# A feed-forward product by seven half-size block products, with loads and gates moved

## The chip, the cores and the metric

One core of one Trainium2 chip runs the whole kernel as one program. The metric is the device time of one execution in microseconds (us). The engines are TensorE (PE), which multiplies matrices into the PSUM banks; VectorE (DVE); ScalarE (ACT); GpSimd (POOL), which has no access to PSUM; and SyncE (SP), which only starts transfers. Each engine has an instruction queue of its own and goes through it in order; waits between engines are semaphores. PEld is the loading of weights into PE, which overlaps the matmuls.

## The reference

Two transformer-like layers over 1024 tokens of width 1024, in float32. What matters here is the first layer:

```python
    xn = _rmsnorm(h, norm_mix_w[l]);  proj = xn @ w_in[l]
    attn = _windowed_gqa(...)         # 8 heads, a band of +-128 keys
    gdn = _gdn_mixer(...)             # gated delta rule in chunks, forward and backward
    h = h + jnp.concatenate([attn, gdn], axis=-1) @ w_out[l]
    hn = _rmsnorm(h, norm_ffn_w[l])
    h = h + jnp.square(jax.nn.relu(hn @ w_ffn_in[l])) @ w_ffn_out[l]
```

Here w_ffn_in is 1024 x 4096 and w_ffn_out 4096 x 1024. The second layer projects its normed input to three branches (pooling, a short convolution, a stick-breaking attention) and to a gate of 3 x 1024 columns; each branch is multiplied with its weights of 512 x 1024, then with sigmoid(gate); the sum goes through w_out_2, a norm, and is added to the layer's input.

## The kernel before

Every matrix operand is held as two float32r tiles, a rounded part H and a remainder L (`split`, L97: ACT casts, DVE or POOL subtracts). A product of a 128x128 block with a 128x512 tile is three matmuls, H.H, H.L and L.H (`mm3`, L146 to L150). Weights come in 256 KB pieces (`weight`, L103): SP loads `raw` (three buffers), ACT casts it, POOL makes the remainder; the w tiles have eight buffers each. `cols` and `rows` cut the weights of a product, `dense` runs one: 24 matmuls fill a PSUM bank, then an epilogue reads it.

The order within an engine's queue is made at build time by a planner that simulates the queues; the order in the program is its priority. Only in the stick-breaking attention is PE's order written out by hand (`turns`, with other products as `fill` between). Loads go through SP's queue (`dma`), most stores through ACT's (`put`). Both are in order: a load that waits for a buffer holds up those behind it. Tile pools are opened and closed in program order, and a new pool may lie over the memory of closed ones; a tile in it waits for the old tiles under it.

The stages in order of time, as far as the change touches them:

- Chunk loop (150 to 260 us). For each of 8 chunks `chunk_of` loads kT and qT, and `decay` loads e, with a copy one chunk ahead. PE transposes kT (L459) and multiplies kT with kT and with qT; ACT and POOL make the decays in e, which has two buffers; the results go to DRAM (`key_d`, `qry_d`). Other projections fill PE.
- Inversion (260 to 331 us). DVE inverts 32x32 blocks row by row (L510, L511), ACT copies X to Xr (L512), four stores bring it to DRAM (L515). PE runs projections.
- Attention and scan (338 to 560 us). The scan's first steps load X and B (L581), then KQ and kv. The attention loads bias (L716), KR (L720) and, per block, R (L729), from which ACT and POOL make Q (L731, L732); L737 is its first matmul. Both run interleaved.
- Output projection (560 to 676 us), which ends with a loop over 8 token tiles in the order 3, 4, 2, 5, 1, 6, 0, 7. Its results `Hs` stay in SBUF.
- Norm and feed-forward (642 to 1345 us). `to_units` scales a token tile (L181), PE transposes it (L184), ACT and DVE split it (L187, L188). Then eight rounds c: the first product for 512 hidden columns, relu and square on ACT (L866, L867), a split (`hid`), and the second product, added to `Hs` on DVE (L881).
- The second layer. Its gate products for the first two branches are fill in the stick-breaking attention and go through DRAM (`ga_d`); 24 parts of the fill are kept back for its end (SPARE). From 2130 us on the three branches follow: y is loaded (`yr`, two buffers) and split, the last branch's gates are computed (two of eight early, the others inside the loop), products and gates are multiplied.
- The last product and norm (2400 to 2472 us): L1282 squares, `rstd_from` makes the factor (L171 to L173), L1292 scales, L1293 adds the residual.

## Time and profile before

| | us |
|---|---|
| median of 3 runs | 2472.67 (2468.53 to 2473.35) |
| profiled execution | 2473.5 |
| its span, from first to last instruction | 2471.7 |
| PE busy | 2357.5 |
| DVE, ACT, POOL busy | 1220.8, 1140.5, 942.1 |

A group of instructions in a profile is named by line of the kernel, engine, operation, and output<-inputs by the program's tile names. Matmuls overlap, so the duration of one is longer than its share of PE's time. PEclk is the granted clock of TensorE as a part of 2.4 GHz.

### The profile page before, as it was taken

To read this page: it belongs to the slowest core of one execution; us is meant where nothing else is said; L and a number is where in the kernel's file an instruction comes from. 1 tells how busy PE (TensorE), PEld (TensorE's weight loads), DVE (VectorE), ACT (ScalarE), POOL (GpSimd) and SP (SyncE) were. 2 spreads that over 40 slices of the span, in tenths; PEclk is the share of its full clock that TensorE was granted. 3 is DMA by queue.
4 is the path that set the end of the run, shared out by engine and by line. 5 is a ranking of instruction groups with operands and counts; after the bars stand their busy time and mean duration, and the time that the engine had idled before them with its cause. 6 is when DMAs were issued, how large, how long until landed. Compare 5 with 4: busy or idle time off the path is not lost. (4 is left out here: it accounts for less than half of the span.)

```text
span 2471.7 us, 31486 instructions
## 1 busy us (share of the span) xinstructions
PE 2357.5 (95%) x11098; PEld 1955.2 (79%) x11098; DVE 1220.8 (49%) x2221; ACT 1140.5 (46%) x2359; POOL 942.1 (38%) x815
## 2 busy tenths in 40 slices
PE   7988978999999999999999999999999999899998
PEld 5776758898788888888888788777887888787887
DVE  4768846975632211221222601887888776432213
ACT  4646335754642232223224522776666788521331
POOL 3445233434522222222213313465445443326454
PEclk9999978999999999999999999999999999999999
DMA  4657774667121111111112324222212332444123
GB/s 133 184 175 219 212 204 137 188 198 239 58 63 54 41 45 52 51 52 52 48 38 81 118 81 129 63 86 77 77 50 72 99 97 85 145 141 145 56 73 124
DMA packets 301137, 262.17 MB, mean 106 GB/s; under 512 B 44871, under 2 KB 236291, under 8 KB 300979
## 3 DMA queue, kind: packets, MB, share of 16 engines
q1 hardware_dynamic: 258131, 207.12, 28.8%
q10 hardware_dynamic: 42848, 53.05, 6.2%
q8 instruction: 87, 1.43, 0.3%
q14 instruction: 71, 0.58, 0.1%
HBM read 197.63 MB, written 64.57 MB: 106 GB/s over the span
## 5 line engine op out<-in xcount | busy, mean ns | idle before, releaser
L99 POOL TENSOR_TENSOR wl<-raw,wh 128x512 fp32r<-128x512 f32 x260 | 349.2, 1355 | 794.2 <-ACT wh L98 784.8
L148 PE MATMUL mm<-uh,wh 128*128 128x512 f32 x1472 | 577.4, 393 | 5.0 <-ACT mx L157 3.5
L150 PE MATMUL mm<-uh,wl 128*128 128x512 f32 x1472 | 575.8, 391 | 0.0
L149 PE MATMUL mm<-ul,wh 128*128 128x512 f32 x1472 | 575.7, 391 | 0.0
L98 ACT CAST wh<-raw 128x512 fp32r<-128x512 f32 x260 | 160.1, 620 | 437.2 <-PE mm L150 235.1
L148 PEld LDWEIGHTS mm<-uh,wh 128*128 128x128 f32 x1472 | 277.4, 189 | 61.5 <-ACT mx L157 3.9
L150 PEld LDWEIGHTS mm<-uh,wl 128*128 128x128 f32 x1472 | 276.9, 188 | 58.9
L149 PEld LDWEIGHTS mm<-ul,wh 128*128 128x128 f32 x1472 | 277.2, 188 | 55.2
L99 DVE TENSOR_TENSOR hid<-t,hid 128x512 fp32r<-128x512 f32 x64 | 55.3, 866 | 302.8 <-ACT hid L98 302.8
L150 PE MATMUL mm<-wh,hid 128*128 128x512 f32 x512 | 199.0, 389 | 0.0
L149 PE MATMUL mm<-wl,hid 128*128 128x512 f32 x512 | 198.8, 389 | 0.0
L148 PE MATMUL mm<-wh,hid 128*128 128x512 f32 x512 | 198.7, 389 | 0.0
L881 DVE TENSOR_TENSOR h<-h,mm 128x512 f32<-128x512 f32 x128 | 87.8, 687 | 213.1 <-PE mm L150 213.0
L1051 POOL TENSOR_TENSOR ul<-u,uh 128x512 fp32r<-128x512 f32 (+3 forms) x96 | 107.7, 1123 | 158.4 <-ACT uh L1050 147.8
L111 POOL TENSOR_TENSOR wl<-raw,wh 128x512 fp32r<-128x512 f32 x88 | 122.4, 1392 | 117.7 <-DVE wh L110 42.8
L148 PE MATMUL mm<-xnh,wh 128*128 128x512 f32 x352 | 142.2, 404 | 9.7 <-ACT t L310 5.5
L149 PE MATMUL mm<-xnl,wh 128*128 128x512 f32 x352 | 140.6, 400 | 0.0
L150 PE MATMUL mm<-xnh,wl 128*128 128x512 f32 x352 | 140.6, 399 | 0.0
L150 PEld LDWEIGHTS mm<-wh,hid 128*128 128x128 f32 x512 | 96.1, 188 | 19.9
L148 PEld LDWEIGHTS mm<-wh,hid 128*128 128x128 f32 x512 | 96.1, 188 | 19.9
L149 PEld LDWEIGHTS mm<-wl,hid 128*128 128x128 f32 x512 | 96.1, 188 | 19.9
L866 ACT ACTIVATE t<-mm 128x512 f32<-128x512 f32 x64 | 38.1, 597 | 143.3 <-PE mm L150 143.3
(336 smaller groups left out, 4625.4 us busy)
## 6 DMA issues: line engine op xcount, KB each, us to landing
raw<-in_w_in SPq DMA_DIRECT2D x172, 256.0 KB
raw<-in_w_ffn_in SPq DMA_DIRECT2D x64, 256.0 KB
raw<-in_w_ffn_out SPq DMA_DIRECT2D x64, 256.0 KB
raw<-in_w_out SPq DMA_DIRECT2D x32, 256.0 KB
kv<-kv_d SPq DMA_DIRECT2D x16, 512.0 KB
ga_d<-mx ACTq DMA_DIRECT2D x32, 256.0 KB
s<-ga_d SPq DMA_DIRECT2D x32, 256.0 KB
raw<-in_w_branch SPq DMA_DIRECT2D x24, 256.0 KB
```

The lines of the kernel that those rows point to most:

```text
L98: act.copy(H, src)
L99: (eng or dve).tensor_sub(L, src, f32(H))
L111: gp.tensor_sub(L, raw, f32(H))
L148: pe.matmul(ps, A[0][:, asl], B[0][:, bsl], start=first, stop=False)
L149: pe.matmul(ps, A[0][:, asl], B[1][:, bsl], start=False, stop=False)
L150: pe.matmul(ps, A[1][:, asl], B[0][:, bsl], start=False, stop=last)
L866: act.activation(t, ps, AF.Relu)
L881: dve.tensor_add(Hs[order[p], n], Hs[order[p], n], ps)
L1051: gp.tensor_sub(uL[:, cs], u[:, cs], f32(uH[:, cs]))
```

## The change

Feed-forward: the normed input, transposed, is cut in four blocks B00, B10 (first 512 tokens, lower and upper half of the 1024 features), B01, B11 (last 512 tokens); 256 columns of the weights likewise in A00, A01, A10, A11, each 512 x 128. Four block products come from seven multiplications with sums of blocks (T1 to T4 of the input, S1 to S4 of the weights). `half` does the first two, which need only the first 512 tokens, `strassen` the other five. Five groups of 16 have their first two done early, one behind each norm tile from the fourth on (`early`). All hidden tiles go to DRAM (`hid_d`), as does the residual (`h_d`). Then the second product runs on its own in eight rounds and reads them back. PSUM has 6 + 2 banks in place of 4 + 2, raw weight buffers are 4 of double size, block tiles have 14 buffers.

Front loads: `front` loads kT, qT and e together, one chunk ahead. Xr is copied on DVE; its stores, the loads of the scan's first step, and the attention's first loads go through ACT's queue. Gates: SPARE is gone; the last branch's eight gate products stand before the products of the branches (two, three and three), and go through DRAM; `yr` has four buffers. Last norm: the weight is multiplied in before the factor is known.

The diff, cut to its core (in the branch stage, `s` has six buffers):

```diff
-    def decay(c):
...
+    def front(c):
+        kT, qT = chunk_of(gk_d, c, "kT"), chunk_of(gq_d, c, "qT")
         e = up_tile("e", 2)
...
         dma(e, g4.partition_broadcast(P))
...
+        return kT, qT, e
+    ahead = [front(0)]
...
-        kT, qT = chunk_of(gk_d, c, "kT"), chunk_of(gq_d, c, "qT")
+        kT, qT, e = ahead.pop()
+        if c < 7:
+            ahead.append(front(c + 1))
...
-        e = decays.pop(c)
-        if c < 7:
-            decays[c + 1] = decay(c + 1)
...
-        act.copy(Xr, X.rearrange("p j i -> p i j"))
+        dve.tensor_copy(Xr, X.rearrange("p j i -> p i j"))
         for b in range(4):
             r = slice(32 * b, 32 * b + 32)
-            dma(xbq_d[0][d].rearrange("c h i j -> (c h) i j")[:, r, r], Xr[r])
+            put(xbq_d[0][d].rearrange("c h i j -> (c h) i j")[:, r, r], Xr[r])
...
-            dma(by_head(t), xbq_d[n][d][c].rearrange("h i j -> i h j"))
+            (dma if step else put)(by_head(t), xbq_d[n][d][c].rearrange("h i j -> i h j"))
...
-        dma(KQ, xbq_d[2][d][c].rearrange("h i j -> i h j"))
+        first = dma if step else put
+        first(KQ, xbq_d[2][d][c].rearrange("h i j -> i h j"))
         kv = ld.tile([P, 2, 512], F32, name="kv", tag="kv", bufs=KV)
-        dma(kv, kv_d[c].rearrange("n i j -> i n j"))
+        first(kv, kv_d[c].rearrange("n i j -> i n j"))
...
-        dma(bias, bass.AP(w.tensor, w.offset + 127, [[511, P], [P * 512, 4], [1, 384]]))
+        first = dma if kv else put
+        first(bias, bass.AP(w.tensor, w.offset + 127, [[511, P], [P * 512, 4], [1, 384]]))
...
-            dma(KR[64 * s : 64 * s + 64], ka_d[kv * 64 : kv * 64 + 64, :])
+            first(KR[64 * s : 64 * s + 64], ka_d[kv * 64 : kv * 64 + 64, :])
...
-                dma(R[64 * s : 64 * s + 64].rearrange("p (h t) -> p h t", h=4), src)
+                (dma if kv or n > 1 else put)(R[64 * s : 64 * s + 64].rearrange("p (h t) -> p h t", h=4), src)
...
+    rwc.close()
+    rw[:] = pool(rwc, "raw2", 4), 1024
...
-    pm[0] = pool(pf, "pff", 4, space=PSUM)
...
+    pm[0] = pool(pf, "pff", 6, space=PSUM)
...
+    h_d, hid_d = scratch("h_d", [T, 1024]), scratch("hid_d", [4096, T])
...
+    xsp = pool(s5, "xs", 14)
...
+    EARLY = 5
...
+    def spare(name):
+        return hp.tile([P, 512], F32, name=name, tag="h")
...
+    B00f, B10f = xtile("x00", F32), xtile("x10", F32)
...
+    def halved(U, cs, src, eng):
+        act.copy(U[0][:, :, cs], src)
+        eng.tensor_sub(U[1][:, :, cs], src, f32(U[0][:, :, cs]))
+    def operand(src, eng):
+        H, L = (wp.tile([P, 512], F32R, name=f"w{q}", tag=f"w{q}", bufs=8).rearrange("p (k m) -> p k m", k=4) for q in "hl")
+        act.copy(H, src)
+        eng.tensor_sub(L, src, f32(H))
+        return H, L
...
+    def accumulate(ps, A, B, first):
+        for k in range(4):
+            for n, (x, y) in enumerate(((0, 0), (0, 1), (1, 0))):
+                pe.matmul(ps, A[x][:, k], B[y][:, k], start=first and k + n == 0, stop=k == 3 and n == 2,
+                          skip_group_check=not first)
...
+    def sums(A, st):
+        A00, A01, A10, A11 = A
+        S1, S2 = st(), st()
+        dve.tensor_add(S1, A10, A11)
+        dve.tensor_sub(S2, S1, A00)
+        return A, S2, operand(S2, dve), operand(S1, dve)
...
+    def half(c0, A00, A01, mu, ht):
+        pa, pb_ = acc512(), acc512()
+        accumulate(pa, operand(A00, gp), B00, True)
+        m1 = mu("m1")
+        act.copy(m1, pa)
+        accumulate(pb_, operand(A01, gp), B10, True)
+        hidden(pb_, m1, c0, 0, ht)
+        return pa
+    def hidden(ps, other, row, h, ht):
+        t = ht("ht")
+        dve.tensor_add(t, other, ps)
+        dve.scalar_tensor_tensor(t, t, 0.0, t, op0=ALU.max, op1=ALU.mult)
+        put(hid_d[row : row + P, 512 * h : 512 * h + 512], t)
...
+    def early(g):
+        if g == 0:
+            W0[:] = A = blocks_of(F1, 0)
+        else:
+            raw = raw_tile().rearrange("p (k m) -> p k m", k=8)
+            dma(raw, F1[:, 256 * g : 256 * g + P].rearrange("(k p) m -> p k m", p=P))
+            A = raw[:, 0:4], raw[:, 4:8]
+        first.append(half(256 * g, *A[:2], spare, spare))
...
+    for p, i in enumerate(order):
...
+        for j in range(2):
+            put(h_d[i * P : (i + 1) * P, 512 * j : 512 * j + 512], hv[j])
+            xs = tmp()
+            dve.scalar_tensor_tensor(xs, hv[j], rs, wb[:, 512 * j : 512 * j + 512], op0=ALU.mult, op1=ALU.mult)
...
+        if p < 4:
+            if p == 0:
+                B00, B10 = pair("b00"), pair("b10")
+            for U, Uf, src in ((B00, B00f, pq[0]), (B10, B10f, pq[1])):
+                act.copy(Uf[:, :, cs], src)
+                halved(U, cs, src, dve)
+            if p == 3:
+                early(0)
...
+        if p == 4:
+            T1, T2, B11, T3, T4 = (pair(n) for n in ("t1", "t2", "b11", "t3", "t4"))
+        b11, t1, t2, t3, t4 = (tx() for _ in range(5))
+        act.copy(b11, pq[1])
+        dve.tensor_sub(t1, pq[0], B00f[:, :, cs])
+        dve.tensor_sub(t3, b11, pq[0])
+        halved(B11, cs, pq[1], dve)
+        gp.tensor_sub(t2, b11, t1)
+        halved(T2, cs, t2, gp)
+        dve.tensor_sub(t4, B10f[:, :, cs], t2)
+        halved(T1, cs, t1, dve)
+        halved(T3, cs, t3, gp)
+        halved(T4, cs, t4, dve)
+        early(p - 3)
+    sums0 = sums(W0, tx)
+    txc.close()
+    hpc.close()
...
+    def strassen(g):
+        c0 = 256 * g
+        if g == 0:
+            pa, ((A00, A01, A10, A11), _, O2, O1) = first[g], sums0
+            S2 = st()
+            gp.tensor_add(S2, A10, A11)
+            gp.tensor_sub(S2, S2, A00)
+        else:
+            A = blocks_of(F1, c0)
+            pa = first[g] if g < EARLY else half(c0, *A[:2], mu, ht)
+            (A00, A01, A10, A11), S2, O2, O1 = sums(A, st)
+        accumulate(pa, O2, T2, False)
+        u2 = mu("u2")
+        act.copy(u2, pa)
+        pc = acc512()
+        accumulate(pc, O1, T1, True)
+        S3, S4 = st(), st()
+        dve.tensor_sub(S3, A00, A10)
+        accumulate(pa, operand(S3, gp), T3, False)
+        u3 = mu("u3")
+        act.copy(u3, pa)
+        hidden(pc, u3, c0 + P, 1, ht)
+        pd = acc512()
+        accumulate(pd, operand(A11, dve), T4, True)
+        hidden(pd, u3, c0 + P, 0, ht)
+        dve.tensor_sub(S4, A01, S2)
+        accumulate(pc, operand(S4, dve), B11, False)
+        hidden(pc, u2, c0, 1, ht)
+    for g in range(16):
+        strassen(g)
+    f1.close()
+    s5.close()
+    rwc.close()
+    ptc.close()
+    pf.close()
...
+    hid = pool(s5, "hid", 22)
+    wbp = pool(s5, "normw", 1)
...
...
-        to_units(hv, rstd_of(hv), p, wb, HU, [pt.tile([P, 512], F32, name="g", tag="g") for _ in range(2)])
...
+    Hs = {}
+    tiles = [(n, p) for n in range(2) for p in range(8)]
...
-        def f1_epi(m, h, ps):
-            t = tmp()
-            act.activation(t, ps, AF.Relu)
-            act.activation(t, t, AF.Square)
-            D[m, h] = tuple(hid.tile([P, 512], F32R, name="hid", tag="hid") for _ in range(2))
-            split(*D[m, h], t)
-        if c == 0:
-            dense(F1, 0, 1, HN, f1_epi, by_half=True)
-        else:
-            for j in range(2):
-                dense(F1, 512 * c + 256 * j, 2, HN, lambda m, h, ps, j=j: f1_epi(2 * j + m, h, ps))
+        for k in range(4):
+            raw = hid.tile([P, 1024], F32, name="hr", tag="hr", bufs=3)
+            dma(raw, hid_d[(4 * c + k) * P : (4 * c + k + 1) * P, :])
+            for h in range(2):
+                D[k, h] = tuple(hid.tile([P, 512], F32R, name="hid", tag="hid") for _ in range(2))
+                split(*D[k, h], raw[:, 512 * h : 512 * h + 512])
...
-        for n, p in [(n, p) for n in range(2) for p in range(8)] if c < 7 else [(n, p) for p in range(8) for n in range(2)]:
...
-            dve.tensor_add(Hs[order[p], n], Hs[order[p], n], ps)
+            if c == 0:
+                Hs[order[p], n] = hp.tile([P, 512], F32, name="h", tag="h")
+                act.copy(Hs[order[p], n], ps)
+            else:
+                dve.tensor_add(Hs[order[p], n], Hs[order[p], n], ps)
...
+        for n, p in tiles[4 * (c - 2) : 4 * (c - 1)] if 2 <= c < 6 else ():
+            r = tmp()
+            dma(r, h_d[order[p] * P : (order[p] + 1) * P, 512 * n : 512 * n + 512])
+            gp.tensor_add(Hs[order[p], n], Hs[order[p], n], r)
...
-    AHEAD, LEAD, SPARE = 16, 24, 24
...
+    AHEAD, LEAD = 16, 24
...
-            while turn[1] and done < LEAD + (t + 1) / len(turns) * (total - LEAD - SPARE):
+            while turn[1] and done < LEAD + (t + 1) / len(turns) * (total - LEAD):
...
-    def gate(gw, h, tag, bufs):
-        s = gt.tile([P, 512], F32, name="s", tag=tag, bufs=bufs)
-        ps = acc512()
-        for k in range(8):
-            mm3(ps, gw(k, 0), HH[k][h], k == 0, k == 7)
-        sigmoid(s, ps)
-        return s
...
-    EARLY = (2, 0), (2, 1)
...
+    BETWEEN = (0, 1), (2, 3, 4), (5, 6, 7)
...
-                raw = gt.tile([P, 512], F32, name="yr", tag="yr", bufs=2)
+                raw = gt.tile([P, 512], F32, name="yr", tag="yr", bufs=4)
...
-        if n == 0:
-            for b, m in EARLY:
-                gw = cols(W2, 5120 + 1024 * b + P * m, 4)
-                for h in range(2):
-                    E[b, m, h] = gate(gw, h, "se", 4)
+        for m in BETWEEN[n]:
+            r = (16 + m) * P
+            gw = cols(W2, 5120 + r, 4)
+            for h in range(2):
+                s = gt.tile([P, 512], F32, name="s", tag="s", bufs=6)
+                ps = acc512()
+                for k in range(8):
+                    mm3(ps, gw(k, 0), HH[k][h], k == 0, k == 7)
+                sigmoid(s, ps)
+                put(ga_d[r : r + P, 512 * h : 512 * h + 512], s)
...
-            ahead = 8 * n + m < AHEAD
-            gw = None if ahead or (n, m) in EARLY else cols(W2, 5120 + 1024 * n + P * m, 4)
...
-                if ahead:
-                    s = gt.tile([P, 512], F32, name="s", tag="s", bufs=4)
-                    r = (8 * n + m) * P
-                    dma(s, ga_d[r : r + P, 512 * h : 512 * h + 512])
-                else:
-                    s = E[n, m, h] if gw is None else gate(gw, h, "s", 4)
+                s = gt.tile([P, 512], F32, name="s", tag="s", bufs=6)
+                r = (8 * n + m) * P
+                dma(s, ga_d[r : r + P, 512 * h : 512 * h + 512])
...
-            rs = rstd_from(zst[:, i])
...
             xr = fo.tile([P, 1024], F32, name="xr", tag="xr", bufs=4)
...
-            for q, eng in ((0, gp), (1, dve)):
+            zw = Z[i], fo.tile([P, 512], F32, name="zw", tag="zw", bufs=2)
+            gp.tensor_mul(zw[0], Z[i], wb[:, 0:512])
+            dve.tensor_mul(zw[1], ps, wb[:, 512:])
+            rs = rstd_from(zst[:, i])
+            for q in (1, 0):
                 c = slice(512 * q, 512 * q + 512)
-                dve.scalar_tensor_tensor(Z[i] if q == 0 else ps, Z[i] if q == 0 else ps, rs, wb[:, c], op0=ALU.mult, op1=ALU.mult)
-                eng.tensor_add(xr[:, c], xr[:, c], Z[i] if q == 0 else ps)
+                dve.scalar_tensor_tensor(xr[:, c], zw[q], rs, xr[:, c], op0=ALU.mult, op1=ALU.add)
```

## Rows read from the trace of the kernel before

**Rows 1.** The page: busy time of PE, share of the span, instructions.

```profile
PE 2357.5 (95%) x11098; PEld 1955.2 (79%) x11098; DVE 1220.8 (49%) x2221; ACT 1140.5 (46%) x2359; POOL 942.1 (38%) x815
```

**Rows 2.** Busy time by stretches; columns stand in the first line.

```profile
core 0: us, PE busy (x) PEld busy (x) DVE busy (x) ACT busy (x) POOL busy (x), PEclk, DMA share, GB/s
150.00:260.00 110.00, 91.78 (x432) 75.03 (x431) 69.67 (x140) 55.73 (x162) 46.95 (x41) 0.92 0.76 213
338.00:352.00 14.00, 1.31 (x6) 0.84 (x6) 0.00 (x0) 4.70 (x5) 6.63 (x7) 0.61 0.96 234
338.00:405.00 67.00, 42.19 (x214) 39.37 (x213) 24.07 (x77) 25.58 (x65) 22.37 (x22) 0.64 0.77 197
405.00:560.00 155.00, 146.45 (x1126) 136.73 (x1125) 129.59 (x378) 101.00 (x248) 64.41 (x65) 1.00 0.64 189
642.00:700.00 58.00, 53.39 (x248) 43.48 (x249) 40.05 (x66) 29.12 (x63) 23.05 (x21) 0.97 0.16 50
700.00:1345.00 645.00, 645.00 (x2853) 534.26 (x2852) 134.18 (x180) 190.35 (x317) 159.72 (x121) 1.00 0.17 50
1540.00:2130.00 590.00, 574.30 (x2587) 469.54 (x2586) 453.34 (x757) 417.81 (x835) 287.35 (x241) 1.00 0.27 82
2130.00:2150.00 20.00, 16.52 (x73) 13.38 (x72) 8.68 (x11) 11.84 (x22) 5.13 (x4) 1.00 0.61 187
2250.00:2270.00 20.00, 14.19 (x57) 10.85 (x57) 6.44 (x8) 3.10 (x5) 14.83 (x12) 0.90 0.44 134
```

**Rows 3.** Groups by line, 700 to 1345 us: busy, mean ns, idle before.

```profile
L99 POOL TENSOR_TENSOR wl<-raw,wh 128x512 fp32r<-128x512 f32 x120 | 159.1, 1342 | 497.9 <-ACT wh L98 495.6 <-PE mm L149 1.4
...
L881 DVE TENSOR_TENSOR h<-h,mm 128x512 f32<-128x512 f32 x113 | 77.6, 687 | 206.3 <-PE mm L150 206.3
L98 ACT CAST wh<-raw 128x512 fp32r<-128x512 f32 x120 | 74.6, 622 | 306.7 <-PE mm L150 235.1 <-DMA raw<-in_w_ffn_in 33.6 <-DMA raw<-in_w_ffn_out 22.9
L99 DVE TENSOR_TENSOR hid<-t,hid 128x512 fp32r<-128x512 f32 x64 | 55.3, 866 | 302.8 <-ACT hid L98 302.8
```

**Rows 4.** PE's waits, whole span: total us, times, longest.

```profile
PE mm L737 <- POOL Q L732: 12.7, 1, 12.7
...
PE g L459 <- DMA kT<-gk_d: 11.0, 4, 3.5
...
PE mm L148 <- ACT y L98: 5.2, 2, 4.5
...
PE g L489 <- DMA qT<-gq_d: 2.8, 1, 2.8
```

**Rows 5.** Waits of SP's queue, 130 to 300 us.

```profile
SPq L443 <- DMA qry_d<-e: 33.8, 6, 10.7
```

**Rows 6.** Timeline of SP's queue, 318 to 366 us: start, duration.

```profile
325.60 12.54 SPq L106 DMA_DIRECT2D raw<-in_w_out  x6
...
342.71 6.48 SPq L515 DMA_DIRECT2D inv_d<-Xr  x4
...
351.53 0.58 SPq L581 DMA_DIRECT2D X<-inv_d  x1
```

**Rows 7.** Timelines of DVE and ACT in the same stretch.

```profile
330.07 1.16 DVE L511 TENSOR_REDUCE X<-M 128x31 f32<-128x961 f32 x1
...
340.76 1.93 ACT L512 COPY Xr<-X 128x1024 f32<-128x1024 f32 x1 [0.40 <-ACT t L535]
```

**Rows 8.** Groups by line, 642 to 700 us.

```profile
L181 DVE SCALAR_TENSOR_TENSOR t<-h,st,wb 128x512 f32<-128x512 f32 x15 | 14.9, 1002 | 6.6 <-issue 4.2 <-PE g L184 1.8 <-POOL st L173 0.7
```

**Rows 9.** Timeline of the end, 2462 to 2472 us.

```profile
2464.02 0.60 ACT L1282 ACTIVATE junk<-mm 128x512 f32<-128x512 f32 x1 [4.75 <-PE mm L150]
...
2465.23 0.55 POOL L173 TENSOR_TENSOR st<-st,cc 128x1 f32<-128x1 f32 x1 [2.73 <-DVE st L172]
2465.82 0.75 DVE L1292 SCALAR_TENSOR_TENSOR z<-z,st,wb 128x512 f32<-128x512 f32 x1 [0.73 <-POOL st L173]
...
2467.28 0.69 DVE L1293 TENSOR_TENSOR xr<-xr,mm 128x512 f32<-128x512 f32 x1
```

79 lines of the change are left out of this document (60 added, 19 removed).

## The prediction

> **What bounds the kernel now.** I read the page's busy table first: TensorE (PE) is busy 95% of the span [rows 1]. Then the busy time by stretches [rows 2]: a share of 95% is a mean over stages with different limits. In the feed-forward stage (700 to 1345 us) PE is busy 645.00 of 645 us, with VectorE (DVE) at 21%. Time is gained there only by fewer matmuls. Elsewhere PE has holes: 18.2 of 110 us from 150 to 260, 12.7 of 14 from 338 to 352, 3.5 of 20 at 2130 and 5.8 of 20 at 2250. Behind the second of these the granted clock is 0.64 over 67 us: part of that stretch ran at 1.2 GHz in place of 2.4. Third, PE's waits say what ended the holes [rows 4]. Fourth, the SyncE (SP) queue says why those loads were late [rows 5, 6].
>
> The price of a matmul is its slot, not the mean duration of a matmul row, since matmuls overlap: 645.00 us / 2853 = 0.2261 us [rows 2].
>
> **Part 1, the first product by seven block products.** Per 256 hidden columns it was 2 x 2 x 8 x 3 = 96 matmuls; now it is 7 products of 12, 84. Over 16 groups 192 matmuls go: 192 x 0.2261 = **-43.4 us**. The second product keeps its 1536. The first then takes 1344 x 0.2261 = 303.9 us of PE, 19.0 a group.
>
> What it adds per group beside PE: ScalarE (ACT) casts 7 operands and copies 3 sums, 10 x 0.622 = 6.2 us [rows 3]. GpSimd (POOL) makes 3 remainders, 3 x 1.342 = 4.0 [rows 3]. DVE makes 4 block sums, 4 remainders and 4 x 2 operations on results, 16 in all. At 0.687 (a sum with a PSUM operand [rows 3]) this is 11.0 us, at 1.002 (the norm's operation from SBUF, with POOL beside it [rows 8]) 16.0; a remainder took 0.866 [rows 3]. So DVE goes from 21% to 58 to 84% of a group, and PE stays the longest by 3 us at least. These operations lie beside the matmuls. What they cost is stalls, since products 3, 5 and 7 add to a bank that ACT or DVE must have read during the one product between. No row shows that wait. Bounds: DVE at 21% goes with no idle PE, at 77% (1540 to 2130) with 15.7 of 590 us or 2.7%, at 84% (405 to 560) with 8.6 of 155 or 5.5% [rows 2]. So 0 to 16.8 us; between, at 2%: **+6**.
>
> The relu and square (two ACT operations) move to one on DVE, counted above. The hidden tiles now go out by 4 puts a group and come back as 512 KB loads, 32 MB more in all over the stage: at most 50 GB/s more than the 50 seen, where 234 GB/s was moved at 338 us [rows 2]. Nothing, covered by that room.
>
> **Part 2, the norm tiles and the early groups.** Before, 642 to 700 us has 4.6 us of idle PE [rows 2]. A tile of the second half now needs 8 DVE operations in place of 4, and 2 more for its early group: 10 x 0.687 to 1.002, four tiles 27 to 40 us [rows 3, 8]. The cover is five early groups of 24 matmuls, 27.1 us. Best case, the old 4.6 go; worst, 40 - 27 = 13 us of new idle PE. T4 has to wait: 16 block tiles share 14 buffers, so it starts when x00 and x10 are done with. It is read by the sixth product only. Much of the work of tiles 4 to 6 can lie under the output projection before it, as the old norm did, so I take **0** (bounds -5 and +13).
>
> **Part 3, between the two products.** Before, the hidden tile never left SBUF. Now the second product starts with four 512 KB reads into buffers that lie over block tiles in use by the last group. At 234 GB/s [rows 2] a read takes 2.2 us, four 9.0, then a cast and a remainder, 1.5 [rows 3]: 10.5 us if all start after the last product, 0 if all fit before. The tiles of the fourth product are free 36 slots or 8.1 us before the end, which leaves 2.4 and something for the buffer that comes last: **+4**. Queued behind such a waiting read on SP are the next weight loads; of those, three raw buffers can be ahead. The residual, now added on POOL from a load, is 16 operations in four of eight rounds of 43 us: nothing.
>
> **Part 4, front loads.** In the chunk loop SP took e, then kT and qT of the next chunk; e waited for the landing of an older e, 33.8 us in six waits [rows 5], and PE waited 11.0 us for kT and 2.8 for qT [rows 4]. Now kT and qT go ahead of that e by one chunk. The wait for e stays (two buffers as before), and the DMA engines are 76% busy there [rows 2]. Bounds 0 and -18.2 (all holes of the stretch); 60% of the 13.8 us: **-8**.
>
> At 338 us: X was ready on DVE at 330.07 + 1.16 = 331.2, but ACT copied it only at 340.76 [rows 7]. Its four stores then took SP from 342.71 for 6.5 us, and the first load of X went out at 351.53 [rows 6]. On DVE the copy follows X at once: 331.2 + 2 + 6.5 = about 340, 11.5 us earlier. The attention's loads (bias, KR, R) stood on SP behind six weight loads that blocked it for 12.54 us to 338.14 [rows 6]; PE waited 12.7 us for what comes of R [rows 4]. On ACT's queue they pass that block. Price: 11.5 us, and some of the half clock after it; all of that would be 0.36 x 42.19 = 15.2 us [rows 2]. Bounds 0 and -27.9. I take **-14**, near the delay that the rows show, since the scan's own latency also leaves PE short there. Cost on ACT: some 20 issues queued in front of its casts; the hole covers them.
>
> The Trainium skill speaks against this part (DMA: Bandwidth & Descriptors, section Issuing engines are not separate DMA queues): transfers started by different engines share the same 16 DMA engines, so that a second issuer saves issue time only. By that the moved loads would save an issue each, some 1 us in place of 14, and the time would be 2421. The rows speak of a queue that stood still for a buffer, which the section leaves out.
>
> **Part 5, gates.** Six gates of the last branch move from inside its loop in front of the second and third branch's products, and the two that stood early stay early; all go through DRAM. Same matmuls. Covered then are the loads of y, with four buffers in place of two: the holes of 3.5 and 5.8 us, ended by y casts (5.2 us [rows 4]), and a clock of 0.90 over 20 us, 2 us [rows 2]. The 24 parts kept back at the end go between the turns, where PE idles 2.7%: nothing. Bounds 0 and -11.3; the wait is a two-buffer one and the cover is 3 x 48 x 0.2261 = 32.6 us, so **-9**.
>
> **Part 6, last norm.** After the last matmul the chain was square, sums, power, two DVE scalings, an add [rows 9]. The scaling by the weight now runs beside the square, and one 0.69 us operation goes: **-0.7** (bounds -1.5, two of 0.75; +0.7, if the product delays the sums).
>
> **Sum.** -43.4 + 6 + 0 + 4 - 8 - 14 - 9 - 0.7 = -65.1. The profiled execution took 2473.5 us (span 2471.7 and 1.8 around it), the median of the runs 2472.67: 2408.4 and 2407.6. Forecast 2408. All bad ends together give -2.4 (2471), all good ones -106.9 (2367).
>
> **Rivals.**
> A, slower: PE starves in the first product. Place: products 3, 5 and 7 of each group. Like 150 to 260 us (PE 83% busy, clock 0.92 [rows 2]) the 303.9 us would take 303.9 / 0.834 / 0.92 = 396, 86 more than forecast: 2494. It decides when a group takes 23.4 us on average ((303.9 + 6 + 65) / 16), as with DVE operations of 1.46 us. For it: DVE at up to 14.0 of 13.6 us in the first five groups (14 operations), while their open sums hold five of six banks. Against: 405 to 560 us, DVE 84%, PE 94% and clock 1.00 [rows 2]. 6%.
>
> The Trainium skill has this as a rule (TensorE: Matmul & The Clock Gate, section A second HAM failure mode: psum-queue depth-cycling): short idles between groups of matmuls that cycle through banks make the clock go up and down. The 645 us stretch cycles through banks at clock 1.00, so the trace bears it out only where PE waits long.
>
> B: the front moves buy nothing, because e and the DMA engines set the pace: 2408 + 8 + 14 = 2430. For it: the 76% and the wait for e. Against: SP's block is seen. 13%.
>
> C: part 1 works, but stalls, norm and passage are at their bad ends: 2408 + 10.8 + 13 + 6.5 = 2438. For it: all three engines busy in the norm tiles. 10%.
>
> D: no new stall, and hole and half clock go: 2408 - 6 - 4 - 4.6 - 10 - 14 = 2369. 10%.
>
> **Numbers.** Forecast (2388 to 2428) 61%, A 6%, B 13%, C 10%, D 10%. Leaving out A, most of D and a little of C, the range is 2375 to 2442. About 0.2% (5 us) is what a measurement here can tell from no change: faster 0.92 (all but A, and 2% of C's tail), same 0.02, slower 0.06.
>
> **What would show it.** Right: 1344 matmuls of the first product at 0.226 us each at clock 1.00, with under 3% idle; PE waiting for no kT; attention's first matmul within 4 us of the last projection; no wait for y over 1 us. Wrong: PE waits in the first product on ACT copies of sums or DVE remainders, 1 us and more per group; half clock there; a hole of over 10 us at the start of the second product; X still late because ACT's own queue holds the stores behind casts that wait for PE.

## The result, and the profile after

The changed kernel takes **2451.1 us** (median of 4 runs, 2447.0 to 2453.5) against 2473.0 beside it (4 runs): ratio 0.9919, 95% interval 0.9901 to 0.9936. It is faster, by 22 us and not by 65; 2451 lies outside the range of 2375 to 2442. The profiled execution took 2453.5 us, its span 2451.5.

The page's busy line, which answers to [rows 1]: TensorE has 192 matmuls less and is busy 37.6 us less, yet the span fell by only 20.2.

```profile
PE 2319.9 (95%) x10906; PEld 1921.2 (78%) x10906; DVE 1423.4 (58%) x2479; ACT 1131.2 (46%) x2365; POOL 967.3 (39%) x829
```

Where the span went is read from distances between instructions that both kernels have (starts and ends of instructions in the two traces, us):

```
                                                      before    after   change
scan's first matmul starts (S)                        357.74   357.74      0.0
S to the end of the output projection's last sum (O)  319.62   315.99     -3.6
O to the first stick-breaking matmul (K)              867.15   854.97    -12.2
K to the end of the last stick-breaking matmul (E)    581.50   604.76    +23.3
E to the end of the last matmul (M)                   337.92   311.15    -26.8
M to the end of the span                                7.79     6.86     -0.9
```

The last three need one remark: 24 parts of three matmuls, 72 x 0.2261 = 16.3 us, moved from behind E to ahead of it. So stick-breaking itself lost 7.0 us and the stage behind it won 10.5.

The stretches of [rows 2], with more of them where the feed-forward part begins (columns: us, PE busy, PEclk, DMA share, GB/s):

```profile
150.00:260.00 110.00, 92.83 (x443) 0.94 0.78 215
338.00:352.00 14.00, 0.00 (x0) 0.50 0.93 209
338.00:405.00 67.00, 39.22 (x226) 0.67 0.78 199
...
1540.00:2130.00 590.00, 571.52 (x2561) 0.99 0.26 78
2130.00:2150.00 20.00, 18.35 (x66) 0.83 0.58 182
2250.00:2270.00 20.00, 20.00 (x90) 1.00 0.50 152
```

```profile
642.00:676.00 34.00, 31.06 (x136) 1.00 0.53 172
676.00:690.00 14.00, 8.46 (x29) 0.51 0.38 109
690.00:724.00 34.00, 29.42 (x145) 1.00 0.21 70
724.00:734.00 10.00, 3.16 (x8) 0.50 0.09 30
734.00:750.00 16.00, 16.00 (x72) 1.00 0.58 179
750.00:1000.00 250.00, 250.00 (x1105) 1.00 0.34 110
1000.00:1050.00 50.00, 43.11 (x181) 0.97 0.52 181
```

In the steady part of the first product (750 to 1000 us) TensorE never idles, and its slot is 250.00 / 1105 = 0.2262 us, the forecast's. But between 642 and 750 us it idles 19.9 us, where it idled 4.6 before [rows 2], and the clock is at 1.2 GHz in two stretches (0.51 and 0.50); around the passage between the two products it idles 6.9. At the front nothing moved: the hole at 338 is still whole, and 150 to 260 has one us less idle.

PE's waits, which answer to [rows 4] (total us, times, longest). The wait for Q has become one for B; the one at L190 is old (12.1 before); the one for kT is there; two new ones, at L896 and the last, stand in the feed-forward part; the wait for y is gone, and one of 9.0 us (1.2 before) stands in stick-breaking. This last one belongs to the gates: it is 2.4 us in e1 and e3 below, which have the old gates, and 8.8 to 9.0 in all the others.

```profile
PE gi L600 <- DMA B<-key_d: 22.5, 2, 21.7
PE g L190 <- DVE t L187: 11.9, 5, 8.1
PE mm L896 <- ACT wh L888: 10.0, 1, 10.0
PE g L468 <- DMA kT<-gk_d: 9.7, 5, 4.3
PE mm L154 <- DVE mx L1299: 9.0, 3, 5.9
...
PE mm L154 <- ACT hid L98: 4.2, 1, 4.2
```

SP's wait for e, which answers to [rows 5], did not shrink:

```profile
SPq L450 <- DMA qry_d<-e: 35.3, 6, 11.3
```

At the hole, where [rows 6, 7] stood: ScalarE's queue, then SP's (start, duration).

```profile
336.48 0.41 ACTq L725 DMA_DIRECT2D bias<-wide_d  x1
...
339.34 0.64 ACTq L738 DMA_DIRECT2D R<-qa_d  x1
340.08 9.60 ACTq L521 DMA_DIRECT2D inv_d<-Xr  x4
...
350.45 0.74 ACTq L587 DMA_DIRECT2D X<-inv_d  x1
```

```profile
322.82 15.88 SPq L112 DMA_DIRECT2D raw<-in_w_out  x8
```

```profile
331.45 1.14 DVE L518 COPY Xr<-X 128x1024 f32<-128x1024 f32 x1
```

The copy of X now runs on VectorE at 331.45 (the last line), but the stores start at 340.08, 2.6 us before those of [rows 6], take 3.1 us longer, and the first load of X goes out at 350.45 against 351.53.

The tail, which answers to [rows 9]: square, sums, power, then two operations of VectorE in place of three.

```profile
2446.23 0.15 DVE L178 TENSOR_SCALAR st<-st 128x1 f32<-128x1 f32 x1
2447.11 0.75 DVE L1484 SCALAR_TENSOR_TENSOR xr<-zw,st,xr 128x512 f32<-128x512 f32 x1 [0.73 <-POOL st L179]
2447.78 0.75 DVE L1484 SCALAR_TENSOR_TENSOR xr<-z,st,xr 128x512 f32<-128x512 f32 x1
```

### The profile page after: what moved, and what is told of

It reads as the page before. It is cut to its first block, busy times and chain, and to the rows that moved or that the text cites. A ratio compares the mean times of both kernels' runs of the same rounds, so it can differ in the third digit from the quotient of the medians.

```text
span 2451.5 us, 31767 instructions
## 1 busy us (share of the span) xinstructions
PE 2319.9 (95%) x10906; PEld 1921.2 (78%) x10906; DVE 1423.4 (58%) x2479; ACT 1131.2 (46%) x2365; POOL 967.3 (39%) x829
## 5 line engine op out<-in xcount | busy, mean ns | idle before, releaser
L99 POOL TENSOR_TENSOR wl<-raw,wh 128x512 fp32r<-128x512 f32 x196 | 264.7, 1362 | 476.2 <-ACT wh L98 417.9
L154 PE MATMUL mm<-uh,wh 128*128 128x512 f32 x960 | 379.7, 396 | 10.2 <-DVE mx L1299 9.0
L156 PE MATMUL mm<-uh,wl 128*128 128x512 f32 x960 | 378.1, 394 | 0.0
L155 PE MATMUL mm<-ul,wh 128*128 128x512 f32 x960 | 377.5, 393 | 0.0
L98 ACT CAST wh<-raw 128x512 fp32r<-128x512 f32 x196 | 119.7, 619 | 290.6 <-PE mm L155 105.9
L154 PEld LDWEIGHTS mm<-uh,wh 128*128 128x128 f32 x960 | 182.1, 190 | 47.8 <-DVE mx L1299 10.3
L156 PEld LDWEIGHTS mm<-uh,wl 128*128 128x128 f32 x960 | 181.7, 189 | 39.4
L155 PEld LDWEIGHTS mm<-ul,wh 128*128 128x128 f32 x960 | 182.0, 190 | 35.8
L117 POOL TENSOR_TENSOR wl<-raw,wh 128x512 fp32r<-128x512 f32 x88 | 121.3, 1379 | 116.5 <-DVE wh L116 34.0
L1223 DVE SCALAR_TENSOR_TENSOR e<-u,e 128x512 f32<-128x512 f32 (+3 forms) x96 | 69.7, 726 | 59.3 <-ACT e L1222 59.0
L888 ACT CAST wh<-sum 128x512 fp32r<-128x512 f32 x62 | 38.2, 621 | 114.8 <-PE mm L896 86.6
```

What stands on the lines that cost most here:

```text
L98: act.copy(H, src)
L99: (eng or dve).tensor_sub(L, src, f32(H))
L117: gp.tensor_sub(L, raw, f32(H))
L154: pe.matmul(ps, A[0][:, asl], B[0][:, bsl], start=first, stop=False)
L155: pe.matmul(ps, A[0][:, asl], B[1][:, bsl], start=False, stop=False)
L156: pe.matmul(ps, A[1][:, asl], B[0][:, bsl], start=False, stop=last)
```

## The experiments

All but e1 start from the changed kernel. Edits move the line numbers by up to eleven. The distances of each profile stand in one table, in us; "time" is the median of the runs, and the second column that of the kernel before beside it. G is the start of ScalarE's copy (u2) of the sum behind group 0's product with T2, F the end of the first product's last matmul. The expectations call that product the second, the prediction numbers it third; some of their figures for G lie up to 1 us ahead of the copy's start.

```
                      time   kernel    S     S-O    O-G    G-F    F-K    K-E    E-M
                             before
changed kernel       2451.1  2473.0  357.7  316.0   62.7  276.9  515.3  604.8  311.2
e1 ffn only          2455.6  2470.4  351.6  315.9   63.8  276.3  516.3  584.8  335.0
e2 old front         2447.7  2470.4  353.8  315.2   64.0  275.8  515.5  602.9  309.5
e3 old gates         2458.2  2470.4  354.0  322.8   62.0  276.8  512.7  587.3  334.5
e4 placement         2448.6  2470.4  354.7  315.8   58.0  275.8  515.5  603.5  309.5
e5 early sums        2457.2  2474.2  354.8  320.3   67.7  276.2  515.5  604.4  309.5
e6 passage           2443.5  2474.2  354.0  319.9   58.2  278.2  514.0  603.3  309.5
e7 split stores      2449.4  2474.2  354.3  318.1   62.8  277.0  515.4  603.4  309.5
e8 e let go early    2445.0  2474.2  345.4  321.5   64.0  277.5  514.6  602.6  309.5
e9 e4 + late T4      2440.5  2472.0  351.4  317.7   53.1  278.3  513.9  603.9  311.1
e10 e6 + early rows  2443.5  2472.0  353.7  325.6   57.8  275.8  509.1  603.8  311.1
e11 late bias        2457.0  2472.0  347.9  330.9   62.7  277.5  515.5  603.9  309.5
e12 changed again    2449.6  2470.0  355.5  318.3   62.7  277.5  514.5  602.9  309.5
e13 together         2427.0  2470.0  344.4  319.2   52.5  278.2  510.5  603.4  309.5
e14 e13 + relu       2427.7  2470.0  344.9  321.9   51.5  278.2  507.9  602.7  309.5
```

Ahead of O the same program differs by up to 6 us from run to run (S is 351.4 to 357.7 in the eight profiles that share the changed front: the first, e3 to e6, e9, e10, e12). From O on, profiles with the same code differ by up to 2.0 us in O-G (62.0 to 64.0), 3.6 in F-K (512.7 to 516.3) and 2.2 in K-E (602.6 to 604.8). So the front is judged by large differences only.

**e1 to e3: which part brought what.** e1 is the kernel before with the feed-forward part alone; e2 and e3 undo one part each, e2 for instance

```
-            put(xbq_d[0][d]....[:, r, r], Xr[r])
+            dma(xbq_d[0][d]....[:, r, r], Xr[r])
```

> Only the feed-forward change on the kernel before: front loads, branch gates and last norm as before. My theory: the front bought about 3 us and gates and last norm about 5, all of them read from checkpoints of the two traces, and the feed-forward part with its norm stage is worth only about 12 us (43 saved in matmuls, 31 given back as idle and half-clock time between the end of the output projection and the first stick-breaking matmul). So this kernel takes about 2461 us, 2457 to 2465. Rival: the feed-forward part is worth the 37 us of the forecast and something in the gates or the front took it back; then this takes about 2436 us. Profile by my theory: the first stick-breaking matmul stands 10 to 14 us ahead of where it was before, and TensorE idles about 20 us more than before between 672 us and 1050 us.

> The changed kernel with the front as before (chunk loads, inversion stores, first loads of the scan and of the attention go back to the SP queue, the transposed copy back to ScalarE). My theory: the front moves bought nothing at the scan's first matmul (357.7 in both) and at most the 3.6 us that show at the end of the output projection; so 2451 to 2456 us. Rival (the forecast): the front is worth 22 us and the loss is elsewhere; then about 2473 us. Profile: the scan's first matmul at 357 to 359 us in either case by my theory; by the rival about 380.

> The changed kernel with the branch gates as before (24 parts spared for after the stick-breaking stage, four gate tiles per branch computed ahead of it); the last norm as changed. My theory: the gates win 10.6 us in the stage after stick-breaking and lose 6.7 in stick-breaking itself; without the change both go: about 2455 us, 2452 to 2458, with the stick-breaking stage back near 586 us and the stage behind it near 338. Rival (the forecast): 9 us for the gates with nothing lost, so about 2460 us. Second rival: the 6.7 us in the stick stage come from elsewhere (the other clock phase, another alignment of the queues), then the stick stage here less its 16.3 us of moved matmuls still stands 6 us over the kernel before and the time is 2461.

e1: 14.7 us under its kernel before (ratio 0.9938, 0.9915 to 0.9961), not 37: the feed-forward part lost its gain by itself, O to K is 10.8 us shorter than before, 12.2 in the first profile. e2: 2447.7 against 2449.6 and 2451.1 for the changed kernel, S within the spread, and O at 667.5 (e1) and 669.0 (e2) with the old front, 669.1 to 679.3 in the eight profiles with the new one: the front moves bought nothing. e3: 7 to 9 us above the changed kernel. With the gates as before, K-E is 17.5 us shorter and E-M 23.4 longer, so the gates won 5.9 against the first profile, and up to 9.8 against the others with the new gates; 16.3 of the 17.5 are the moved matmuls. But K-E is still 3.3 us (e1) and 5.8 (e3) above the 581.5 of the kernel before, with the old gates in both: there the second rival was right, and the 6.7 us of my theory are not the gates'. The rows say where they come from. K to E, the kernel before and e3:

```profile
1544.50:2126.00 581.50, 565.80 (x2549) 1.00 0.26 80
1528.30:2115.60 587.30, 571.83 (x2549) 0.99 0.26 79
```

e3 has as many matmuls and no more idle, but TensorE is busy 6.0 us longer: the clock is at 0.50 in four stretches, 13.6 us together, and never in the kernel before. In e1 1.7 us of busy time and 1.6 of idle make the 3.3. Behind E both are 3.0 and 3.4 us shorter than the kernel before, so that from K to the last matmul they lose 0.4 (e1) and 2.4 (e3).

**e4: placement.** The scheduler gave the first-half tiles memory that the output projection holds to its end. ScalarE's timeline of the changed kernel: the copies of the first norm tile (L964) stand behind weight casts (L888) that wait for the projection's last matmuls.

```profile
668.28 0.62 ACT L888 CAST wh<-raw 128x512 fp32r<-128x512 f32 x1 [1.89 <-PE mm L156]
...
672.67 0.57 ACT L964 COPY x<-g 128x512 f32<-128x512 f32 x1
```

```
-    xsp = pool(s5, "xs", 14)
+    xlo = pool(s5, "xlo", 6)      # x00, x10, B00, B10; T4 takes the slots of x00, x10
+    xsp = pool(s5, "xs", 8)
...
```

> The changed kernel with one edit: the tiles of the first half of the tokens (two unsplit, four split halves) have a pool of their own that lies below the pool of the second half's tiles. In the changed kernel they lie over memory that the output projection reads until it ends (150 to 182 KB of a partition), here over memory that is free by then. My theory: the placement is what puts the PSUM copies of the first norm tiles behind the early weight casts on ScalarE and with them behind the output projection's last matmuls; here two of the four first tiles are copied while the projection still runs, the first early matmul starts at 677 to 680 instead of 685.65, and the time falls by 5 to 10 us, to 2441 to 2446. Rival: the round trip through two PSUM buffers and VectorE's order set the pace of the first four tiles; then the first early matmul stays within 2 us of 685 and the time within 2 us of 2451.

ScalarE's timeline of this run: two tiles are copied under the projection.

```profile
657.56 0.59 ACT L965 COPY x<-g 128x512 f32<-128x512 f32 x1
...
665.49 0.58 ACT L965 COPY x<-g 128x512 f32<-128x512 f32 x1
...
666.43 2.21 ACT L889 CAST wh<-raw 128x512 fp32r<-128x512 f32 x4
```

The first early matmul starts 5.7 us behind O instead of 11.9 and O-G is 58.0 instead of 62.7: the placement's price is 4.7 us at G (5.9 over O to F), at the low end of the theory. The median (2448.6) is too near to show it by itself; the distances show it, and e6, e9, e10 repeat the early start (5.2 to 5.7 us behind O).

**e5: the 10.0 us wait.** The sums of group 0, last in VectorE's row, moved ahead of four tiles:

```
             if p == 3:
                 early(0)
+                sums0 = sums(W0, tx)
...
-    sums0 = sums(W0, tx)
```

> The changed kernel with one edit: the two sums of weight blocks of group 0 (and their two split operands) stand right behind the first early group, four norm tiles earlier; in the changed kernel they are the last of VectorE's work in the norm stage, and TensorE waits 10.0 us for the cast of them, until 730.84. My theory: that wait is only the place of two sums in VectorE's row; T2 of the last tile is complete at 724.4, so the wait shrinks by 5 to 8 us, the first copy behind group 0's second product comes 56 us behind the output projection's last sum instead of 62.2, and the time falls by about 6 us. Rival: VectorE's 35 us of work for the four second tiles set the end whatever the order; then the copy stays at 61 to 63 us behind and the time does not move. The weight casts of groups 1 and 2 then also stand behind the first tiles' copies on ScalarE, which may give 2 to 5 us at the first early matmul as well (11.9 us behind the output projection's last sum in the changed kernel).

The theory fell. PE's waits from 660 to 760 us in this run:

```profile
PE mm L896 <- DVE ht L931: 5.5, 2, 3.1
PE g L958 <- DVE tx L975: 4.2, 1, 4.2
PE g L958 <- DVE b00l L884: 1.5, 1, 1.5
```

The 10 us wait is gone and others stand in its place; O-G is 5 us longer. A wait for the last of a full row of work is not removed by another order of the row. In the changed kernel, VectorE is busy 29.73 of the 31 us from 700 to 731.

**e9: less in the row.** On the kernel of e4, T4 is formed behind the sums, not tile by tile:

```
-        dve.tensor_sub(t4, B10f[:, :, cs], t2)
+        late.append((cs, t2, t4))       # both old lines stand for all four tiles behind sums0
...
-        halved(T4, cs, t4, dve)
```

> The kernel of the placement run with one more edit: the fourth combination of the second-half tiles (subtraction, rounded half, remainder: 8 VectorE and 4 ScalarE instructions) is formed for all four tiles behind the sums of group 0 and not tile by tile; nothing reads it before group 0's sixth product. My theory: VectorE's instructions for the four second tiles set the end of the norm stage (moving the two sums of group 0 ahead of them took away the 10 us wait and gave it back in other waits), so 8 instructions of 0.68 us less ahead of it bring the copy behind group 0's second product from 57 us to 51 to 53 us behind the output projection's last sum. Rival: the waits of the early groups on PSUM, casts and transposes set the pace; then the copy stays at 56 to 58 us. Time: 4 to 6 us under the placement run by the theory, the same by the rival.

O-G 53.1: 4.9 us less than e4, near 8 x 0.68 = 5.4; over O to F it is 2.4 us less, since part of the work comes back behind G. PE's wait there went from 9.9 in e4 to

```profile
PE mm L897 <- ACT wh L889: 5.5, 1, 5.5
```

The edit also moves four casts of ScalarE, but ScalarE is busy only 14.70 of the 32 us from 690 to 722 here and VectorE 29.14. So VectorE's row is the likely bound of the norm stage's second half.

**e6 and e10: between the products.** e6 fixes the order of all split tiles in memory, so that the first rows read back lie over T2 and T1 and not over B11; e10 adds

```
+        if g == 13:
+            for k in range(2):
+                for h in range(2):
+                    pre[k, h] = fp.tile([P, 512], F32, name="pre", tag="pre", bufs=4)
+                    dma(pre[k, h], hid_d[k * P : (k + 1) * P, 512 * h : 512 * h + 512])
```

> The changed kernel with every half of a split tile in a place of its own: first-half tiles lowest (as in the run on placement), then the tiles in such an order that the first rows read back for the second product come to lie over T2 and T1, whose last use is 8 to 11 us ahead of the end of the first product, instead of over B11, which is used last. My theory: the read-back at 1013.17 waits for B11's last matmul, and the 6.9 us of TensorE idle between the products, with 3.4 us at half clock behind it, come from that; here the first read-back is issued up to 2.4 us earlier (the weight loads ahead of it on SP's queue end at 1010.8) and the idle falls to 3 to 5 us. Rival: the read-back is held by SP's weight loads alone, which wait for the first product's weight tiles; then the idle stays within 1 us of 6.9. In the norm stage as with the placement run: first early matmul 5 to 7 us behind the output projection's end instead of 11.9. Time: 6 to 9 us under the changed kernel, 2440 to 2446.

> The kernel of the passage run with the first two of the four row blocks that the second product needs first read back during group 14 of the first product, into four tiles of their own, ahead of the weight loads on SP's queue. The passage run showed that the place of the split tiles alone does nothing (6.93 us idle). My theory: the read-back stood behind SP's ten weight loads, which wait for weight tiles that the first product holds to its end; two blocks are now there in time, the other two still come behind the weight loads: 3 to 5 us idle between the products instead of 6.9. Rival: the casts of the rows on ScalarE stand behind the last weight cast of the first product (1013.18) and set the first matmul whenever the rows come; then 6 to 7 us stay.

e6: the read-back goes out 2.5 us ahead of F instead of 0.2. TensorE's waits from 990 to 1050 us add up to 6.9 as before; the one between the products fell only from 4.2 to 3.4.

```profile
PE mm L154 <- ACT hid L98: 3.4, 1, 3.4
```

My theory fell; the rival's number is right but not its reason, since SP was earlier. ScalarE's row stood idle on VectorE's last hidden tile, whose store is queued ahead of the cast, until 1013.00:

```profile
1013.00 1.14 ACT L98 CAST hid<-hr 128x512 fp32r<-128x512 f32 x2 [2.29 <-DVE ht L933]
```

e10: the casts follow the last weight cast at once, the wait between the products is 1.0 us in place of 3.4 (4.2 in the changed kernel), the idle from 1000 to 1050 us is 3.7 (6.0 in e6, 6.9 in the changed kernel), with no half clock there, and F-K is 509.1, 4.9 less than e6.

```profile
1012.64 0.62 ACT L98 CAST wh<-raw 128x512 fp32r<-128x512 f32 x1 [3.60 <-PE mm L897]
1013.16 1.13 ACT L98 CAST hid<-pre 128x512 fp32r<-128x512 f32 x2
```

```profile
1000.00:1050.00 50.00, 46.30 (x203) 1.00 0.54 175
```

**e7 and e11: the hole at 338.** e7 gives two of each four stores to SP; e11 holds the attention's first loads back until the scan's first blocks have landed:

```
+            for (x, b), z in zip(gate, hold):
+                gp.tensor_tensor(z, x[:, 0:1], b[:, 0:1], op=ALU.add)
+            gp.tensor_tensor(bias[:, 0, 0:1], hold[0], hold[1], op=ALU.add)   # also KR, R
```

> The changed kernel with the four stores of each inverted block shared between the queues: two on ScalarE's, two on SP's. In the changed kernel the four take 8.1 to 9.6 us of ScalarE's queue and the scan's first matmul stands 17.7 us behind the start of the first of them in three runs alike. My theory: what the hole ahead of the scan waits for is issue time on a queue that is let go only when TensorE's last weight tiles are free, not the inversion; with two stores on each queue the first matmul stands 12.5 to 14 us behind the start of ScalarE's first store and the time falls by 4 to 5 us. Rival: SP's eight weight loads (15.88 us, ended at 338.7) hold its two stores as long as ScalarE's row held the other two, so that X comes no earlier; then the distance is 16 to 18 us and nothing moves. Second rival: the load of B that ends the wait takes 6.5 us to land whatever is ahead of it.

> The changed kernel with the attention's first loads (bias of 768 KB, key rows of 512 KB, first query rows of 256 KB) held back until the first two blocks of the scan have been read: three one-column writes that depend on those blocks stand ahead of the loads. In the changed kernel the 16 DMA engines are 0.85 to 1.2 busy through the hole from 340 to 357.74, and these 1.5 MB lie ahead of the inversion's stores on ScalarE's queue. My theory: not the choice of queue but this traffic, and its issues ahead of the stores, set the hole (kernel before, changed kernel and the run with split stores all show 17.7 us from the first store's start to the scan's first matmul, 15 to 18 with the stores on SP); without it 10 to 13 us, the first store within 1 us of the last projection cast, and the scan 4 to 9 us earlier. Rival: the distance is the issue time of stores of 128-byte rows and the landing of the block loads; then 15 us or more stay. At the end of the output projection I expect 2 to 6 us of it, since the attention's first scores then come later.

e7, SP's queue and then ScalarE's: SP's two stores begin at 336.59, ScalarE's two only at 342.38.

```profile
336.59 5.09 SPq L521 DMA_DIRECT2D inv_d<-Xr  x2
```

```profile
342.38 1.64 ACTq L521 DMA_DIRECT2D inv_d<-Xr  x2
```

The scan's first matmul stands 11.9 us behind ScalarE's first store, but 17.7 behind the first store of all, where the changed kernel and seven runs with its front have 16.9 to 18.3: nothing gained. e11, ScalarE's queue:

```profile
335.19 4.08 ACTq L521 DMA_DIRECT2D inv_d<-Xr  x4
339.31 1.00 ACTq L587 DMA_DIRECT2D X<-inv_d  x1
...
368.73 0.37 ACTq L732 DMA_DIRECT2D bias<-wide_d  x1
```

Without that traffic the four stores take 4.1 us instead of 9.6, and the scan starts 12.7 us behind the first store (17.7 in the changed kernel; 15.0 in the kernel before, not 17.7 as the expectation has it): my theory of the hole holds. But S-O grows to 330.9, and the time is 6 to 7 us above the changed kernel. The attention's scores are what TensorE does beside the scan; the first of them came at 386.0 (second line below) instead of 362.8 (first line, changed kernel), and in between they were missing.

```profile
362.81 0.58 PE L746 MATMUL mm<-KH,Q 128*128 128x256 f32 x1 [0.42 <-POOL Q L741]
```

```profile
386.02 0.36 PE L757 MATMUL mm<-KH,Q 128*128 128x256 f32 x1
```

I had expected 2 to 6 us of gain at O: wrong.

**e8: the chunk loop.** The second product goes to a tile of b's ring, so that e is free when VectorE has read it, not when its store has landed:

```
-            dve.tensor_mul(e[:, d], kq, e[:, d])
-            put(xbq_d[2][d][c]..., by_head(e[:, d]))
+            dve.tensor_mul(b2[:, d], kq, e[:, d])
+            put(xbq_d[2][d][c]..., by_head(b2[:, d]))
```

> The changed kernel with the second product of the chunk loop written into a tile of its own ring (that of b) and not back into e, so that the load of the next-but-one chunk's decays waits for VectorE's product and not for the store's landing. My theory: e paces the loop (33.8 us of waits on SP in the kernel before, and the early loads of kT and qT changed nothing because they stand behind e in the same row); here TensorE's waits for kT (9.7 us in 5) fall below 5 us, TensorE is busy 95 to 98 of the 110 us from 150 to 260 (92.83 in the changed kernel), and the scan starts 3 to 6 us earlier. Rival: TensorE's idle there is the projections' own (VectorE's convolutions), and b's ring now waits in e's place; then the busy time stays within 1.5 us of 92.8 and nothing moves or it gets slower by up to 5 us.

```profile
150.00:260.00 110.00, 97.58 (x473) 0.95 0.82 230
```

```profile
PE g L468 <- DMA kT<-gk_d: 4.0, 4, 3.1
```

TensorE is busy 4.75 us more in the stretch than in the changed kernel (90.4 to 93.7 in all profiles without this edit), the scan starts at 345.4 (in no other run with that front code below 351.4) and O comes at 666.9 (669.1 at the earliest with that front code, 673.8 in e12). e paced the loop. Not all of the gain at S is the loop's: the attention's first load goes out 6.6 us ahead of the first inversion store here (3.6 in the changed kernel), the four stores take 5.6 us instead of 9.6, and the scan stands 12.9 us behind the first of them. The hole shrinks as in e11, without holding a load back.

**e12 to e14: together.** e13 joins e8, e10 (with e6) and e9's late T4; e14 also squares the early groups' positive part on ScalarE (`act.activation(t, t, AF.Relu)`, then `AF.Square`).

> The changed kernel unaltered, beside the two kernels that follow, so that they can be set against it on one chip. 2447 to 2453 us; the distances between checkpoints as in its first profile to 1 us from the output projection's end on (62.2 us to the copy behind group 0's second product, 515 us from the end of the first product to the stick-breaking stage), and 4 us or more off ahead of it, since the runs so far differ by up to 6 us at the scan's start with the same program there.

> The changed kernel with the edits that showed a gain in one stage each: the decays' tile let go early (scan start 8 to 12 us earlier, output projection's end 4 to 7), first-half tiles in memory that is free early (5 us), the fourth combination formed late (4 us), the first two row blocks read back early (5 us). My theory: the stages stand one behind the other and TensorE sets each, so the gains add: 17 to 21 us under the changed kernel, 2428 to 2434 us. Rival: they overlap or the gain ahead of the scan is given back by the output projection's end, as in the run with the late bias; then 12 to 15 us, 2434 to 2440.

> The kernel with all gains, with one more edit: in the five early groups the square of the positive part is formed by two ScalarE instructions instead of one VectorE instruction. My theory (VectorE's row sets the norm stage: 29.1 of 32 us busy from 690 to 722 in the run with the late fourth combination): five instructions of 0.68 us less on VectorE give 1.5 to 3 us there, the copy behind group 0's second product at 50 to 51.5 us instead of 53. Rival: the wait that is left is for ScalarE's casts (5.5 us), and ten more instructions of 0.6 us on ScalarE make it longer; then 53 to 56 us.

e13 takes **2427.0 us** (2426.3 to 2430.8), ratio 0.9825 (0.9809 to 0.9841), 22.6 under the changed kernel beside it, a little more than I expected. Against e12 the scan starts 11.1 us earlier and O comes 10.2 earlier, O-G is 10.2 and F-K 4.0 shorter: the losses are separate and add. e14: O-G 51.5, one us less and within the spread, and a time that can't be told from e13's: neither theory nor rival is borne out. In the 25 us ahead of G, VectorE is now busy 18.85 us (22.27 in e13), so its row no longer bounds the stage by itself; what does stays open.

## Why the prediction was wrong

**Part 1, the matmuls: right.** 192 slots of 0.2262 us. The stalls that I put at +6 did not come: 250.00 of 250 us busy, VectorE at 60% (150.38 us), the low end of 58 to 84%. Rival A is refuted.

**Part 2, norm tiles and early groups: the step that failed most.** I took 0 because "much of the work of tiles 4 to 6 can lie under the output projection". Nothing of it did: not even the first tile was copied before 672.67, and of the 64 transposes of the norm tiles 8 stand ahead of O, where 24 did before. Measured are +15.3 us of idle (19.9 less 4.6), above my bound of 13, and half clock beside it, a cost that my sum of this part did not have: 14 us at 0.51 and 10 at 0.50 with 11.6 us of busy TensorE in them. O to K lost 43.4 - 12.2 = 31.2 us of the gain in all; 15.3 here and 6.9 at the passage are idle, so 9.0 are left. Half clock makes some 7.2 of them: from O to K TensorE is busy 17.9 us at a clock of 0.50 (3.4 before), and half of the difference is lost. The 16 transposes that now stand behind O are the likely rest. Two causes of the idle are shown, placement (4.7 us, e4) and T4 in VectorE's row (4.9, e9; 5.9 and 2.4 if read over O to F); with VectorE busy 29.73 of 31 us, what failed was not the count of its work but its cover. The rule of the Trainium skill that I weighed under rival A (TensorE: Matmul & The Clock Gate, section A second HAM failure mode: psum-queue depth-cycling) names short idles between groups of matmuls as what brings the clock down and up. The trace agrees with it: the clock fell to 0.51 and 0.50 in the norm stage, where TensorE waited 1.2 to 10 us between groups, and stayed at 1.00 in the product, where it did not wait from 750 to 1000 us.

**Part 3, the passage: near in size, not in cause.** +4 forecast; 4.2 and some half clock measured (6.9 with two waits inside the last group). The cause that I gave, buffers over block tiles in use, was worth under 1 us (e6): what mattered stood ahead in the rows of SP and ScalarE (e10).

**Part 4, the front: -22 forecast, nothing measured.** The chunk loads: my -8 took 60% of PE's waits although I wrote that the wait for e stays. It stayed (35.3 us), and e8 shows that it was the pace. The hole: I put the stores at 331 + 2 and forgot what stands ahead of them on ScalarE's queue, the bias, key and query loads that the same change had put there, and casts that wait for TensorE; it is the last point of my list of what would show me wrong. And the price was wrong beyond that: in e11 the scan started 4 to 10 us earlier than in the eight profiles with the new front, and the time rose. The section of the Trainium skill that spoke against this part (DMA: Bandwidth & Descriptors, Issuing engines are not separate DMA queues: a second issuer saves issue time only) holds here: the DMA share from 338 to 352 is 0.93 here and 0.96 in [rows 2], and between the first store and the scan lie 15.0 us with the stores on SP's queue (kernel before), 17.7 on ScalarE's and 17.7 on both (e7). Rival B was right about the front.

**Part 5, the gates: near.** 10.5 won in its stage (-9 forecast, bound -11.3); against e1 and e3, with the old gates but the new feed-forward part, 7 to 9. "Nothing" for the 24 parts in stick-breaking was right for the gates: K-E is 15.3 to 17.5 us longer with them than in e3, and 16.3 of it are the moved matmuls. The +7.0 against the kernel before, which no term of the sum held, is more idle (3.4 us, 2.3 in e12) and half clock (17.0 us of it in the first profile, 13.7 in e12, none before; e3 has 13.6 without the gates). Why the clock falls there with the new feed-forward part, which ends 500 us before, no run shows; it stays open.

**Part 6: right**, -0.9 for -0.7.

**The sum.** -43.4 + 15.3 + 9.0 + 6.9 - 3.6 + 7.0 - 10.5 - 0.9 = -20.2, where the -3.6 ahead of O lie within that stretch's spread. Of the 44.9 us between this and -65.1, the norm stage is 24.3, the front 18.4, gates and stick-breaking 5.5, the passage 2.9; the stalls that did not come give 6 back, the tail 0.2. Rival B described the front, and rival C the norm stage and the passage, though not the stalls; I had priced them as alternatives, and both came.

## What to carry to other kernels

Before a stage's new work is costed at nothing because it can lie under the stage before, look where its tiles lie: memory that the earlier stage holds to its end shuts that cover, whatever the engines have free. A wait for the last item of a full row of an engine goes away by taking work out of the row (e9), not by another order of it (e5), and a transfer moved to another queue still waits for what stands ahead of it on that queue. A hole that is closed by delaying other work counts only if that work was not the filler of what follows (e11).

## What the runs showed of the hardware

Four stores of 128 KB in rows of 128 bytes took 8.0 to 9.6 us of ScalarE's queue when the attention's first load had gone out 2.9 to 4.2 us ahead of them (eight profiles), 5.6, 5.2 and 4.3 us at 6.6, 6.9 and 8.0 us ahead (e8, e13, e14), and 4.1 us without those loads (e11); on SP's queue, at 4.3 to 4.5 us ahead, 6.5 to 7.1 (kernel before, e1, e2). So how long an issue holds its queue went mostly with the traffic beside it. TensorE's clock can fall in a stage that a change leaves alone: K to E had no half clock before and 13.6 us of it in e3. And one program's front differs by 6 us between executions while its later stages repeat to 2 to 4 us, so that an edit ahead of O has to be worth more than that, or be shown by a distance inside its own stage.
